# Hybrid encoder block on one core: operand sums and late low parts on GpSimd, query loads on ScalarE's queue

## Chip, core and metric

The kernel runs on one core of a Trainium2 chip. The metric is the device time of one execution in microseconds (us); smaller is better. Engines are named as in the profile: PE (TensorE matmuls), PEld (its weight loads), DVE (VectorE), ACT (ScalarE), POOL (GpSimd) and SP (SyncE, which only issues DMAs here).

## What is computed

One layer of a hybrid encoder on 2048 tokens of width 1024, all in float32:

```python
xn = rms_norm(h, ln_mix_g); proj = xn @ w_in
y_a = mlstm_group(...)          # 4 heads x 128, bidirectional, chunks of 128
y_b = mla_group(...)            # latent attention, 4 heads, scores 192 wide, values 128
h = h + concat([y_a, y_b]) @ w_out
u = dwconv3_centred(rms_norm(h, ln_ffn_g) @ w_up, conv_w, conv_b)   # 1024 -> 2 x 2816
gate, val = split(u); h = h + (silu(gate) * val) @ w_down            # 2816 -> 1024
gate = sigmoid(rms_norm(h, ple_norm_g) @ w_ple_gate)
h = h + gate * rms_norm(p @ w_ple_proj, ple_post_g)
out = rms_norm(h, final_g)
```

## The kernel before

Every float32 operand of a large product is split into a high part (ACT, `nc.scalar.copy` to fp32r, L117) and a low part (source minus high part, on DVE, L120). A product is three matmuls: low x high, high x low, high x high (`mm3`, L128, whose matmuls all carry the line L130).

The stages follow each other: the input projection; attention with the mLSTM interleaved as side work; the output projection; up and down; the per-layer input embedding (ple).

**Attention** (`attend_begin`, `attend`). 64 tiles of 128 queries, 16 for each head. A query tile pair (256 queries) is loaded from DRAM into `q_t` by `load_q` (L895), one of two places in turn, and split by `split_q`. The load is written at the start of an odd tile for the pair after next; its place is free when the last score matmul (L917) of the pair before has run. For a tile, five matmuls make each of four score banks, DVE takes their maxima (L918) and the maximum of those (`nm`, L929, L930), ACT the exponentials (L936), PE transposes them (L976), and they are split into `pt` for the product with the values. mLSTM work runs on all engines between these steps.

**Up and down** (`up_down`, L1376). Both products are done by a Strassen-Winograd scheme with seven products for a 2 x 2 block: A11 B11, S1 T1, S2 T2, A12 B21, S3 T3, A22 T4, S4 B22. A "pair" is one pass over these: 44 pairs for up (22 column blocks of gate and value, for two blocks of 1024 tokens), 24 for down (8 pairs of token tiles, for three blocks of the inner width). So there are five blocks; pairs 0, 22, 44, 52 and 60 begin one. The B and T operands (tile `op`, places x0 to x15) belong to a block and are loaded anew at its start by `load_op` (L1258): a DMA into one of six places t0 to t5 in turn (`opr`), then a split. B11, T1, T2, B21 and T3 are loaded during the last pair of the block before; T4 and B22 in the block's first pair, since the old ones are needed until then. Each has four parts (three in the last block).

The T operands are sums and differences of B parts. `sum4` (L1222) makes them: four loads (`tsum`, places t0 to t3), four subtractions (L1232 to L1235), and four stores to DRAM. `sums(0)` does this in the output projection for the first block of tokens and also splits three results in place; `sums(1)` for the second block of tokens (4 steps); `wsums` for the three blocks of w_down (11 steps).

In a pair the order is: A11 B11; S1 T1; `rest` of the pair before (A22 T4, then S4 B22); S2 T2; A12 B21; S3 T3. The results go through PSUM tiles `fxy` (x and y) and `fzs` (z and a spare bank): several products accumulate onto the same bank after DVE has added the partial result elsewhere (`add`, L1380), so PE waits for such additions. In up the results land in `ug` and `uv`, then `conv` (DVE, ACT) makes the gated hidden values, which go to DRAM. In down they are added into two output tiles `fh` (`s.o[0]`, `s.o[1]`), loaded by `down_out` from h1 or h2 in DRAM and stored back. Pair 44 (`NUP`), the first of down, takes its second output tile in the place `u2`, where `uv` of the last pair of up was.

**Last transposes.** The last token tile of the output projection is normalized (`norm_load`, L1070) and left pending; `turn(s, f)` (L1447) transposes half of it into the spare bank of a pair, copies it by ACT, and with the second half stores it to x2 in DRAM.

The program is written with a framework that assigns semaphores and, for the engines' queues, an order: it simulates the instructions with a cost model and takes the first ready one by the order of the text. So instructions can stand earlier in a queue than the text has them (the sums do), and each queue is then worked off strictly in that order, a waiting instruction holding up those behind it. All DMAs are issued by SP.

```python
if i == 1:
    turn(s, 1)
if prev:
    rest(prev)
...
if i == 0:
    turn(s, 0)
...
if i == NUP:
    c22 = self.at("t7", [P, SB], name="c22")
    add(c22, s.p1, s.y)
    add(c22, c22, s.z)
    s.o += self.down_out(NUP, (1,))
    add(s.o[1][:, L], s.o[1][:, L], s.p1)
    add(s.o[1][:, H], s.o[1][:, H], c22)
```

Of the kernel before, what the change touches and what calls it, by code (L numbers as in the profile page):

```python
# [14 lines left out]
ALU = mybir.AluOpType  # L15
# [33 lines left out]
def _f(ap):  # L49
    return ap.bitcast(F32)  # L50
# [10 lines left out]
class Block:  # L61
# [826 lines left out]
    def attend_begin(self):  # L888

        nc = self.nc  # L890
# [3 lines left out]

        def load_q(h, pr):  # L895
            q = self.at(f"w{4 - pr % 2}", [P, 4, 256], F32R, "q_t")
            nc.sync.dma_start(_f(q[:, 2:4]), self.q_d[h, pr])
            qv[h, pr] = q

        def split_q(h, pr):  # L900
# [293 lines left out]
    NUP = 2 * NC2  # L1194
# [27 lines left out]
    def sum4(self, src, dst, ops):  # L1222
        nc = self.nc
        r = []
        for i in range(4):
            r.append(self.at(f"t{i}", [P, SB], name="tsum"))
            nc.sync.dma_start(r[i], src(i))
        b11, b12, b21, b22 = r
        tt = nc.vector.tensor_tensor
        if ops:  # L1230
            self.split(b11, *ops["B11"])
        tt(b12, b12, b11, op=ALU.subtract)  # L1232
        tt(b22, b22, b12, op=ALU.subtract)
        tt(b11, b22, b11, op=ALU.subtract)
        tt(b21, b21, b22, op=ALU.subtract)  # L1235
        if ops:
            self.split(b12, *ops["T1"])
            self.split(b22, *ops["T2"])
        for i, t in enumerate((b12, b22, b11, b21)):
            if not ops or i > 1:  # L1240
                nc.sync.dma_start(dst(i), t)
# [16 lines left out]
    def load_op(self, blk, n):  # L1258

        ops = self.xop[n] = self.op_places(blk, n)  # L1260
        for k, (hi, lo) in enumerate(ops):
            raw = self.at(next(self.orot), [P, SB], name="opr")
            if blk < 2:
                if n[0] == "T":
                    src = self.t_d[blk, int(n[1]) - 1, :, k]
                else:
                    o = blk * 2 * SB + (int(n[2]) - 1) * SB
                    src = self.x2_d[:, (int(n[1]) - 1) * 4 + k, o:o + SB]
            elif n[0] == "T":
                src = self.tw_d[blk - 2, int(n[1]) - 1, :, k]  # L1270
            else:
                src = self.w_down(blk - 2, k, 2 * (int(n[1]) - 1) + int(n[2]) - 1)
            self.nc.sync.dma_start(raw, src)
            self.split(raw, hi, lo)

    def up_load(self, i):

# [98 lines left out]
    def up_down(self, out):  # L1376
# [19 lines left out]
        def rest(s):  # L1396

            prod(s.y, s.ops["A22"], "T4", True)
            if s.down:
                add(s.o[1][:, L], s.o[1][:, L], s.y)  # L1400
                nc.sync.dma_start(self.h2_d[2 * s.pr + 1], s.o[1])
            else:
                add(s.uv[:, 2:2 + SB], s.p1, s.y)
            prod(s.z, s.ops["S4"], "B22", True)
            if s.down:
                add(s.o[0][:, H], s.o[0][:, H], s.z)
                nc.sync.dma_start(self.h2_d[2 * s.pr], s.o[0])
            else:
                add(s.ug[:, 2 + SB:2 + 2 * SB], s.ug[:, 2 + SB:2 + 2 * SB], s.z)
# [37 lines left out]
        def turn(s, f):  # L1447

            xn, otag, dst = self.pending
            if f == 0:  # L1450
                self.pend_o = self.at(otag, [P, KT, P], name="nt_o")
            pt = s.spare.rearrange("p (k t) -> p k t", t=P)
            for j in range(4):
                kt = f * 4 + j
                nc.tensor.transpose(pt[:, j, :], xn[:, kt * P:(kt + 1) * P], self.ident)
            nc.scalar.copy(self.pend_o[:, f * 4:f * 4 + 4], pt)
            if f:
                nc.sync.dma_start(dst, self.pend_o)
# [6 lines left out]
        for i in range(n):  # L1465
# [32 lines left out]
            load(then, "T1")  # L1498
            side(7)
            if i == 1:  # L1500
                turn(s, 1)
            if prev:
                rest(prev)
            if j == 0 and blk:
# [4 lines left out]
            if s.down:  # L1509
                add(s.o[0][:, H], s.o[0][:, H], s.y)  # L1510
            else:
                s.ug = self.at(f"u{i % 2}", [P, 2 * SB + 2], name="ug")
                add(s.ug[:, 2 + SB:2 + 2 * SB], s.p1, s.y)
            if i == 0:
                load(0, "T3")
            load(then, "T2")
# [9 lines left out]
            else:  # L1526
                nc.scalar.copy(s.ug[:, 2:2 + SB], x)
            side(7)
            if i == 0:
                turn(s, 0)  # L1530
            if prev and not prev.down:
                conv(prev)
            if i == NUP - 1:
# [4 lines left out]
            if i == NUP:  # L1538
                c22 = self.at("t7", [P, SB], name="c22")
                add(c22, s.p1, s.y)  # L1540
                add(c22, c22, s.z)
                s.o += self.down_out(NUP, (1,))
                add(s.o[1][:, L], s.o[1][:, L], s.p1)
                add(s.o[1][:, H], s.o[1][:, H], c22)
                outs[i + 1] = self.down_out(i + 1)
            elif s.down:
                add(s.o[1][:, H], s.o[1][:, H], s.y)
                add(s.o[1][:, H], s.o[1][:, H], s.z)
            else:
                s.uv = self.at("u2", [P, 2 * SB + 2], name="uv")  # L1550
                add(s.uv[:, 2 + SB:2 + 2 * SB], s.p1, s.y)
                add(s.uv[:, 2 + SB:2 + 2 * SB], s.uv[:, 2 + SB:2 + 2 * SB], s.z)
# [198 lines left out]
```

## Time and profile before

| | us |
|---|---|
| median of 3 runs (2986.38 to 2987.69) | 2986.76 |
| profiled execution | 2983.04 |
| its span, first to last instruction | 2981.2 |
| PE busy | 2917.6 |
| DVE busy | 2068.2 |
| ACT busy | 1349.0 |
| POOL busy | 141.2 |

The span is 1.8 us shorter than the time of the same execution, which also holds what lies around it. The mean granted clock of TensorE is 0.997. Shares of busy time are means over stages with different limits; the waits of one engine for another and the time line of a stage tell what holds it up. The releaser named in a wait is the one that came last by the profile.

### The profile page before, as it was taken

To read this page: it belongs to the slowest core of one execution; us is meant where nothing else is said; L and a number is where in the kernel's file an instruction comes from. 1 tells how busy PE (TensorE), PEld (TensorE's weight loads), DVE (VectorE), ACT (ScalarE), POOL (GpSimd) and SP (SyncE) were. 2 spreads that over 40 slices of the span, in tenths; PEclk is the share of its full clock that TensorE was granted. 3 is DMA by queue.
4 is the path that set the end of the run, shared out by engine and by line. 5 is a ranking of instruction groups with operands and counts; after the bars stand their busy time and mean duration, and the time that the engine had idled before them with its cause. 6 is when DMAs were issued, how large, how long until landed. Compare 5 with 4: busy or idle time off the path is not lost. (4 is left out here: it accounts for less than half of the span.)

```text
span 2981.2 us, 40678 instructions
## 1 busy us (share of the span) xinstructions
PE 2917.6 (98%) x14858; PEld 2454.1 (82%) x14858; DVE 2068.2 (69%) x3799; ACT 1349.0 (45%) x2646; POOL 141.2 (5%) x262
## 2 busy tenths in 40 slices
PE   8999999999999999999999999999999999999999
PEld 7888888888898888888788888777887787877887
DVE  7431556777777777646798888877778777687565
ACT  7221545555665566523544445444445222233444
POOL 3100000000000000001000000000000000000111
PEclk9999999999999999999999999999999999999999
DMA  6522445343333343568663435786435556575221
GB/s 191 114 73 92 138 131 156 119 144 98 103 106 97 94 126 107 160 218 284 212 223 130 141 134 184 254 254 201 126 121 184 193 192 227 175 244 203 80 80 64
DMA packets 377400, 460.19 MB, mean 154 GB/s; under 512 B 30176, under 2 KB 263152, under 8 KB 377200
## 3 DMA queue, kind: packets, MB, share of 16 engines
q1 hardware_dynamic: 377200, 457.59, 48.1%
q8 instruction: 117, 1.92, 0.3%
q14 instruction: 83, 0.68, 0.1%
HBM read 294.26 MB, written 163.25 MB: 153 GB/s over the span
## 5 line engine op out<-in xcount | busy, mean ns | idle before, releaser
L130 PE MATMUL fxy<-op,fw 128*128 128x512 f32 x3168 | 752.8, 394 | 22.8 <-DVE fh L1380 13.0
L130 PEld LDWEIGHTS fxy<-op,fw 128*128 128x128 f32 x3168 | 588.3, 188 | 170.3 <-DVE fh L1380 23.4
L130 PE MATMUL fzs<-op,fw 128*128 128x512 f32 x1584 | 385.8, 389 | 0.8 <-DVE xt L1151 0.8
L130 PEld LDWEIGHTS fzs<-op,fw 128*128 128x128 f32 x1584 | 297.1, 188 | 63.0 <-DVE xt L1151 1.0
L130 PE MATMUL bk<-wsp,xh 128*128 128x512 f32 (+1 forms) x768 | 235.1, 387 | 1.0 <-DVE wsp L126 1.0
L117 ACT CAST pt<-tb 128x512 fp32r<-128x512 f32 x256 | 146.4, 586 | 194.2 <-PE tb L976 193.7
L918 DVE TENSOR_REDUCE mx<-bk 128x1 f32<-128x512 f32 x256 | 174.5, 684 | 45.4 <-PE bk L917 44.5
L130 PE MATMUL ppv<-pt,kv 128*128 128x256 f32 x1536 | 203.1, 287 | 0.0
L130 PE MATMUL fxy<-op,fwd 128*128 128x512 f32 x792 | 191.5, 390 | 6.0 <-DVE uv L1380 4.1
L120 DVE TENSOR_TENSOR pt<-tb,pt 128x512 fp32r<-128x512 f32 x256 | 173.7, 685 | 33.9 <-ACT pt L117 32.4
L130 PEld LDWEIGHTS ppv<-pt,kv 128*128 128x128 f32 x1536 | 188.7, 191 | 0.4 <-ACT pt L117 0.4
L936 ACT ACTIVATE pe<-bk,nm 128x512 f32<-128x512 f32 x256 | 174.2, 695 | 25.4 <-DVE nm L930 24.4
L130 PEld LDWEIGHTS fxy<-op,fwd 128*128 128x128 f32 x792 | 148.0, 188 | 39.0 <-DVE uv L1380 5.3
L130 PE MATMUL pgp<-pw,x3s 128*128 128x512 f32 (+1 forms) x792 | 178.5, 384 | 0.0
L130 PE MATMUL bk<-wo,yhl 128*128 128x512 f32 x744 | 175.6, 392 | 0.0
L130 PEld LDWEIGHTS bk<-wsp,xh 128*128 128x128 f32 x768 | 145.4, 190 | 27.3 <-DVE wsp L126 2.2
L130 PEld LDWEIGHTS pgp<-pw,x3s 128*128 128x128 f32 x792 | 144.5, 188 | 28.3
L1380 DVE TENSOR_TENSOR fh<-fh,fxy 128x512 f32<-128x512 f32 (+1 forms) x139 | 104.8, 768 | 86.0 <-PE fxy L130 84.8
L130 PEld LDWEIGHTS bk<-wo,yhl 128*128 128x128 f32 x744 | 138.2, 188 | 28.1
L130 PE MATMUL bk<-wsp,xl 128*128 128x512 f32 (+1 forms) x384 | 151.4, 394 | 7.9 <-DVE xl L120 7.9
L130 PE MATMUL bk<-xh,wqk 128*128 128x512 f32 x480 | 157.2, 393 | 0.0
L117 ACT CAST fw<-hraw 128x1024 fp32r<-128x1024 f32 (+1 forms) x72 | 70.3, 980 | 184.8 <-PE fxy L130 116.1
(331 smaller groups left out, 5020.5 us busy)
## 6 DMA issues: line engine op xcount, KB each, us to landing
fwr<-in_w_up SPq DMA_DIRECT2D x66, 512.0 KB, 4.2
fh<-h_d SPq DMA_DIRECT2D x48, 512.0 KB, 4.8
h_d<-fh SPq DMA_DIRECT2D x48, 512.0 KB, 2.8
s_d<-fwr SPq DMA_DIRECT2D x44, 512.0 KB, 3.2
fws<-s_d SPq DMA_DIRECT2D x44, 512.0 KB, 3.9
rw<-row_d SPq DMA_DIRECT2D x32, 512.0 KB, 5.1
hraw<-hid_d SPq DMA_DIRECT2D x30, 512.0 KB, 4.7
tsum<-in_w_down SPq DMA_DIRECT2D x44, 256.0 KB, 4.0
```

Of the source, the lines that this page charges most:

```text
L117: nc.scalar.copy(hi, src)
L120: (sub or nc.vector).tensor_tensor(lo, src, _f(hi), op=ALU.subtract)
L130: mm = lambda *a, **k: self.nc.tensor.matmul(*a, **k, skip_group_check=more)
L918: nc.vector.tensor_reduce(s.mx[:, kb:kb + 1], ps, axis=AX.X, op=ALU.max)
L936: nc.scalar.activation(s.pe[:, kb % 2], s.banks[kb], AF.Exp, bias=s.nm, scale=ASCALE, accum_out=s.rs[:, kb:kb + 1])
L1380: add = lambda o, a, b: tt(o, a, b, op=ALU.add)
```

## The change

Five parts. (a) `load_q` issues its DMA from ACT in place of SP. (b) The subtractions of `sum4` run on GpSimd, except those of `sums(0)`. (c) The low parts of T4 and B22 are made on GpSimd in all blocks but the first. (d) The two halves of the last transposes move from pair 0 (after A12 B21) and pair 1 (after S1 T1) to pair 1, after S1 T1 and after S2 T2. (e) In pair 44 the second output tile is no longer added to in the pair itself: in `rest`, DVE adds the product A22 T4 to `p1`, and GpSimd adds `p1` and `c22` to the two halves of the tile, which is then stored.

```diff
         def load_q(h, pr):
             q = self.at(f"w{4 - pr % 2}", [P, 4, 256], F32R, "q_t")
-            nc.sync.dma_start(_f(q[:, 2:4]), self.q_d[h, pr])
+            nc.scalar.dma_start(_f(q[:, 2:4]), self.q_d[h, pr])
...
-        tt = nc.vector.tensor_tensor
+        tt = (nc.vector if ops else nc.gpsimd).tensor_tensor
...
-            self.split(raw, hi, lo)
+            self.split(raw, hi, lo, sub=self.nc.gpsimd if blk and n in ("T4", "B22") else None)
...
             prod(s.y, s.ops["A22"], "T4", True)
-            if s.down:
+            if s.i == NUP:
+                add(s.p1, s.p1, s.y)
+                for f, t in ((L, s.p1), (H, s.c22)):
+                    nc.gpsimd.tensor_tensor(s.o[1][:, f], s.o[1][:, f], t, op=ALU.add)
+                nc.sync.dma_start(self.h2_d[1], s.o[1])
+            elif s.down:
                 add(s.o[1][:, L], s.o[1][:, L], s.y)
...
             if i == 1:
-                turn(s, 1)
+                turn(s, 0)
             if prev:
                 rest(prev)
...
                 add(s.ug[:, 2 + SB:2 + 2 * SB], s.p1, s.y)
+            if i == 1:
+                turn(s, 1)
...
             side(7)
-            if i == 0:
-                turn(s, 0)
...
                 add(c22, c22, s.z)
                 s.o += self.down_out(NUP, (1,))
-                add(s.o[1][:, L], s.o[1][:, L], s.p1)
-                add(s.o[1][:, H], s.o[1][:, H], c22)
+                s.c22 = c22
                 outs[i + 1] = self.down_out(i + 1)
```

## The prediction

> **What bounds the kernel now.** I read the page's busy times first, then the waits of PE, longest first, then busy times by stage, then the time line around the stages in which PE stands idle.
>
> ```profile
> span 2981.2 us, 40678 instructions
> PE 2917.6 (98%) x14858; PEld 2454.1 (82%) x14858; DVE 2068.2 (69%) x3799; ACT 1349.0 (45%) x2646; POOL 141.2 (5%) x262
> ```
>
> PE is idle for 2981.2 - 2917.6 = 63.6 us. The change removes no matmul, so that is all it can win, apart from clock. Who ends the idle time (total, times, longest):
>
> ```profile
> PE fxy L130 <- DVE fh L1380: 13.3, 8, 4.7
> PE fxy L130 <- DVE ug L1380: 6.2, 5, 1.8
> PE bk L913 <- ACT pe L936: 4.6, 4, 2.6
> PE fxy L130 <- DVE fw L120: 2.4, 1, 2.4
> PE fzs L1455 <- DVE xt L1070: 2.0, 1, 2.0
> ```
>
> The rows with fxy and fzs are up and down, where DVE empties the banks of PSUM; bk L913 is attention. In stages (busy us of PE, PEld, DVE, ACT, POOL, then the granted clock):
>
> ```profile
> 1432.00:1850.00 418.00, 415.20 (x1818) 336.95 (x1818) 352.12 (x454) 194.70 (x262) 0.73 (x2) 1.00 0.50 170
> 1850.00:1900.00 50.00, 43.94 (x189) 34.71 (x188) 44.81 (x60) 27.60 (x41) 0.00 (x0) 1.00 0.78 255
> 1900.00:2050.00 150.00, 143.13 (x621) 115.15 (x620) 122.63 (x158) 61.79 (x81) 0.00 (x0) 1.00 0.78 250
> 2050.00:2250.00 200.00, 200.00 (x881) 164.78 (x880) 145.39 (x170) 88.87 (x115) 0.00 (x0) 1.00 0.42 130
> 2250.00:2340.00 90.00, 80.15 (x336) 64.34 (x335) 78.38 (x108) 45.45 (x68) 0.00 (x0) 0.96 0.66 211
> 2340.00:2742.00 402.00, 396.80 (x1727) 319.80 (x1726) 298.58 (x418) 116.64 (x158) 1.49 (x5) 1.00 0.61 204
> 1024.00:1036.20 12.20, 11.76 (x68) 10.36 (x69) 8.25 (x23) 7.66 (x25) 1.20 (x2) 0.86 0.33 98
> 2332.60:2343.50 10.90, 10.90 (x41) 8.64 (x42) 7.96 (x10) 2.10 (x2) 0.00 (x0) 0.85 0.76 254
> ```
>
> In the first block of up (1432 to 1850) DVE is busy for 352.12 of 418 us, 84%, and PE loses 2.8 us. Between 1850 and 2050 DVE is as busy, 167.4 of 200 us, and PE loses 6.06 + 6.87 = 12.9. A high load of DVE alone does not stop PE; that DVE stands still, or does its work in the wrong order, does. PE is idle for 9.85 us from 2250 to 2340 (the first pairs of down) and for 5.2 after that. The last two rows begin at or near the end of a PE gap of 2.58 and 3.57 us (quoted below). Their granted clock is 0.86 and 0.85, so such a gap costs another 12.2 x 0.14 = 1.7 or 10.9 x 0.15 = 1.6 us.
>
> **Query loads on ScalarE's queue.** SP issues this load, 32 times, behind whatever its queue holds. Once it came late:
>
> ```profile
> 1016.55 0.32 SPq L812 DMA_DIRECT2D rw<-row_d  x1
> 1017.08 0.32 SPq L897 DMA_DIRECT2D q_t<-q_d  x1
> 1023.30 0.40 ACT L117 CAST q_t<-q_t 128x256 fp32r<-128x256 f32 x1 [3.19 <-DMA q_t<-q_d]
> 1024.44 0.50 PE L913 MATMUL bk<-kv,q_t 128*128 128x512 f32 x1 [2.58 <-ACT pe L936]
> ```
>
> All waits of ACT for it, all landings that the trace tells, and ACT's waits for the scores' maximum nm:
>
> ```profile
>   DMA q_t<-q_d: 8.0, 8
> DMA to landing us min/median/max: 2.4/2.6/4.9
> ACT pe L936 <- DVE nm L930: 24.4, 31, 1.8
> ```
>
> The load landed 6.2 us after its issue, against a median of 2.6, one place behind a larger transfer of the same queue. ACT stood at the cast of q_t, the exponentials behind it came late, and PE waited 2.58 us. In all ACT waits 8.0 us for this load. If all four waits of bk L913 (4.6 us) have this cause and the clock's 1.7 is added, 6.3 us can be won. Against it stands ACT's own time: 0.32 us an issue on SP, x 32 = 10.2 us at the most. Most of it falls where ACT waits anyway, 24.4 us in 31 cases, for nm before the first exponential of a tile; without that cover it would delay the exponentials one for one. The load waits for the last score matmul of a tile; queued behind it on ACT are the casts of the probabilities and the mLSTM activations, for which DVE and PE wait. The next exponential needs that matmul too, so the wait is short. SP's queue loses that wait, and its mLSTM loads go out earlier. Bounds: -6.3 to +10.2; I take -4.0, nearer to the row that shows the loss. The Trainium skill ("DMA: Bandwidth & Descriptors", Issuing engines are not separate DMA queues) says that DMAs of all issuing engines run on the same 16 DMA engines and that another engine saves only the time to initiate them. By that rule this term is about zero and the sum 4 us higher; no run here has a load on ACT's queue.
>
> **Last transposes moved.** PE's 2.0 us at fzs L1455 go: at pair 1 the normalized rows are long there, and PE passes at once to the next product. What is late next: the store of x2 goes out 36 matmuls, some 8 us, later, and loads for the sums queued behind it on SP wait for its landing; they are wanted only at pair 21. -2.0, with +2 as the other bound should a weight load be queued behind that wait.
>
> **Sums by way of DRAM on GpSimd.** 4 + 11 steps of 4 subtractions, 60 in all, leave DVE. Its waits for them, between 1432 and 2750, and the duration of one:
>
> ```profile
> DVE tsum L1232 <- DMA tsum<-in_w_down: 6.8, 4, 3.8
> DVE tsum L1232 <- DMA hid_d<-fgv: 3.7, 1, 3.7
> DVE tsum L1233 <- DMA tsum<-in_w_down: 2.8, 2, 2.0
> DVE tsum L1235 <- DMA tsum<-in_w_down: 1.6, 2, 0.9
> L1233 DVE TENSOR_TENSOR tsum<-tsum x19: 681/685/695, 1358.6 to 2042.2; 128x512 f32<-128x512 f32 x19
> ```
>
> One case in the time line, and PE behind it:
>
> ```profile
> 2042.18 0.69 DVE L1233 TENSOR_TENSOR tsum<-tsum 128x512 f32<-128x512 f32 x1 [2.04 <-DMA tsum<-in_w_down]
> 2047.13 1.21 PE L130 MATMUL fxy<-op,fwd 128*128 128x512 f32 x4 [1.32 <-DVE uv L1380]
> ```
>
> DVE stands still 14.9 us for loads (6.8 + 3.7 + 2.8 + 1.6), and with it the additions that free the banks. On GpSimd only GpSimd waits. Of the 6.87 us from 1900 to 2050 I take back 5.0. The results are needed at the next block, over 100 us later, so a slower GpSimd is hidden here.
>
> **Low parts of T4 and B22 on GpSimd.** 8 + 8 + 8 + 6 = 30 subtractions leave DVE at the four changes of block. There they stand ahead of additions that PE needs:
>
> ```profile
> 1869.52 3.69 DVE L120 TENSOR_TENSOR op<-opr,op 128x512 fp32r<-128x512 f32 x6
> 1873.13 0.68 DVE L1380 TENSOR_TENSOR ug<-p,fxy 128x512 f32<-128x512 f32 x1
> 1873.86 0.96 PE L130 MATMUL fxy<-op,fw 128*128 128x512 f32 x3 [1.16 <-DVE ug L1380]
> ```
>
> and, in the first pair of down,
>
> ```profile
> 2306.84 1.28 DVE L120 TENSOR_TENSOR op<-opr,op 128x512 fp32r<-128x512 f32 x2
> 2308.04 0.68 DVE L1380 TENSOR_TENSOR fh<-fh,fxy 128x512 f32<-128x512 f32 x1
> 2308.78 10.22 PE L130 MATMUL fxy<-op,fw 128*128 128x512 f32 x36 [4.72 <-DVE fh L1380]
> ```
>
> One takes 3.69 / 6 = 0.615 us in a row. At 1869 all six are of this kind: the gap of 1.16 goes, and half of the 2.4 us for fw, behind two others: -2.4. At 2306, by the order of the loads, three are: 3 x 0.615 brings the gap from 4.72 to 2.9: -1.8. In the later blocks (5.2 us idle) I take -1.0.
>
> **The first pair of down.** Its second output tile is loaded late, and DVE waits for it:
>
> ```profile
> 2330.61 0.69 DVE L1380 TENSOR_TENSOR fh<-fh,p 128x512 f32<-128x512 f32 x1 [1.44 <-DMA fh<-h_d]
> 2331.83 1.27 DVE L1380 TENSOR_TENSOR fh<-fh,fxy 128x512 f32<-128x512 f32 x2
> 2332.56 2.92 PE L130 MATMUL fxy<-op,fw 128*128 128x512 f32 x6 [3.57 <-DVE fh L1380]
> ```
>
> After the change DVE adds the product to p1, which needs no load, and GpSimd adds to the tile. Without the wait of 1.44 and the two additions ahead (2 x 0.615) the bank is free 2.7 us earlier; the rest of the gap is DVE's order, of which I take 0.4. With the clock's 1.6: -4.7. The tile's store goes out a little later, and is read a block later.
>
> **What GpSimd costs DVE.** 92 additions or subtractions run there (60 + 30 + 2). Before, it ran one operation of this size, with one tensor read, and DVE ran against it:
>
> ```profile
> L835 DVE TENSOR_TENSOR qi<-qk,rw x32: 664/916/1048, 659.8 to 1197.0; 128x512 f32<-128x512 f32 x32
> L830 POOL TENSOR_SCALAR_AFFINE_SELECT mk<-rw x32: 634/638/1168, 663.4 to 1195.7; 128x512 f32<-128x512 f32 x32
> ```
>
> Each slows the other: 664 becomes 1048 ns, 634 becomes 1168. With two tensors GpSimd's operation lies between 0.64 us and twice that, 1.28; I take 1.2. A DVE operation behind it then loses up to 0.38 + 0.56 = 0.94 us, against 0.615 saved; nothing when DVE is idle or, as I assume, has one of its inputs in PSUM. For 32 of the 92, at changes of block, the excess is 32 x 0.33 = 10.4 us at the most, and I charge half, 5.0. For the 60 sums it is 60 x 0.33 = 20 us spread over up, where DVE has 16% free; I charge 3.0. Bounds: 0 to 30. The Trainium skill ("SBUF — State Buffer", on the engine ports) says that a DVE instruction with two SBUF inputs and a GpSimd instruction that reads SBUF exclude each other for the whole instruction, that the later one blocks, and that a DVE instruction with only one SBUF input does not contend; the two rows agree with the first, and none of them shows the last. Its "GPSIMD Engine Reference" (Performance versus the Vector engine) advises DVE for elementwise work and gives 4497 ns for 2048 columns, from which 1.12 us for 512 is an estimate; by it the charge would be slightly smaller.
>
> **The sum.** -4.0 - 2.0 - 5.0 - 2.4 - 1.8 - 1.0 - 4.7 = -20.9; + 8.0; so about -13.0 us. The profiled execution took 2983.04 us (span 2981.2) and should take 2970.0 (span 2968.2). The median of the runs is 2986.76, 3.7 above the profiled one: 2973.8.
>
> **Rivals.** (1) *The low parts come late.* T4 and B22 are wanted one pair later, some 72 matmuls, at 200 us / 881 = 0.227 us, 16.3 us. Eight on GpSimd take 8 x 1.2 = 9.6; if each waits behind a DVE operation (0.68) they take 15.1, and with landing and cast they are late. It decides from about 1.9 us each. At 3 us late in four changes of block, with the clock's 1.6 each, it costs 18.4, and the 5.2 won there are lost: -13.0 + 23.6 = +10.6, 2997.4, slower. For it: 1168 is measured for one input. Against it: half of DVE's work there reads PSUM. (2) *The blocking eats the gain.* With all of the 20.9 charged in place of 8 (the bound is 30) the time is 2986.8, no change. For it: 1048 against 664 when the two meet. Against it: 84% load of DVE cost PE nothing in the first block. (3) *Hardly any blocking*, and the query loads win all: -20.9 - 2.3 = -23.2, 2963.6. (4) *The queue of ACT brings nothing* (the same DMA engines, the same landing): 2977.8, inside the forecast.
>
> **Numbers.** Forecast (with 4) 0.56, (1) 0.16, (2) 0.17, (3) 0.11. A measurement tells 0.2%, 6 us, from no change. Faster: 0.56 + 0.11 = 0.67; same 0.17; slower 0.16. The range is 2963.5 to 2990: it leaves out (1) and the far end of (3).
>
> **What would show it.** Right: no PE wait at L1455; no DVE wait on tsum; PE's gap near 2332 under 1 us; POOL's busy time up by 92 x 1.2 = 110 us; ACT's wait for q_t near zero. Wrong: POOL operations of 2 us and more with PE waiting for op behind them; DVE subtractions of 1.2 us in place of 0.69 in up; new waits of bk on ACT in attention.

## The result, and the profile after

| | before | after |
|---|---|---|
| median of runs side by side, us | 2986.57 (2982.27 to 2987.69) | 3034.72 (3029.95 to 3039.51) |
| profiled execution, us | 2983.04 | 3031.74 |
| its span, us | 2981.2 | 3029.9 |

The change makes the kernel slower: the ratio of after to before is 1.0164, interval 1.0143 to 1.0185, some 48 us where 13 us less were forecast. The parts of the change keep the letters of the section on the change: (a) query loads, (b) sums, (c) low parts, (d) last transposes, (e) first pair of down.

The first part of the page of after:

```profile
span 3029.9 us, 40705 instructions
PE 2940.3 (97%) x14858; PEld 2469.4 (82%) x14858; DVE 2069.9 (68%) x3707; ACT 1349.1 (45%) x2646; POOL 298.4 (10%) x354
```

DVE has 92 instructions less and is busy for as long as before (2068.2). POOL is busy for 157.2 us more; over 92 operations that is 1.7 us each. PE stands idle for 3029.9 - 2940.3 = 89.6 us, 26.0 more than before, and is itself busy for 22.7 us more with the same 14858 matmuls. The second goes with the clock. The slow spell behind one gap of PE, of which more below (length, busy us of PE, PEld, DVE, ACT, POOL, granted clock, DMA share, GB/s):

```profile
1485.43:1488.84 3.41, 3.41 (x10) 2.63 (x9) 0.47 (x2) 0.19 (x1) 0.02 (x1) 0.50 0.94 319
```

After a gap of 3.61 us the clock is 0.50 for 3.41 us and then full again (1.00 from 1488.84 on), which costs 1.7 us. So the clock adds to what such a gap costs.

The stages below are bounded by the same matmuls before and after, counted by their number. After: attention, the first block of up, and the part of the second block in which the sums for down are made; then the last two before:

```profile
479.68:1237.85 758.17, 741.30 (x4926) 664.53 (x4925) 551.06 (x1399) 452.00 (x1212) 44.16 (x62) 0.99 0.36 114
1437.89:1871.81 433.92, 422.35 (x1817) 340.92 (x1816) 354.31 (x438) 193.76 (x262) 30.56 (x18) 0.98 0.48 163
1925.19:2092.45 167.26, 149.47 (x621) 119.95 (x619) 113.59 (x116) 60.96 (x80) 61.55 (x39) 0.95 0.71 232
```

```profile
1432.14:1849.96 417.82, 415.02 (x1818) 336.81 (x1817) 352.08 (x454) 194.66 (x262) 0.73 (x2) 1.00 0.50 170
1900.11:2050.02 149.91, 143.04 (x620) 115.08 (x619) 122.52 (x158) 61.79 (x81) 0.00 (x0) 1.00 0.78 250
```

Against before: attention +6.1 us, first block of up +16.1, the change to the second block +3.2, the sums for down +17.4, the first pairs of down +1.3 and the rest of down +4.7. The two large ones are where the sums run on POOL (30.56 and 61.55 us busy). In the rest of up POOL does nothing, and it took as long as before (199.7 us).

The waits of PE after:

```profile
PE fxy L130 <- ACT ug L1534: 18.6, 8, 4.9
PE fxy L130 <- DVE uv L1380: 10.7, 3, 4.3
PE bk L913 <- ACT pe L936: 9.1, 5, 2.9
```

The wait at the transposes (L1455 before) is gone, as intended. No row says that PE waits for an operand that GpSimd made. What PE waits for is VectorE's and ScalarE's emptying of PSUM, later than before. There are two ways to this. The first, by VectorE, shows at the gap named above:

```profile
1475.06 1.30 POOL L1232 TENSOR_TENSOR tsum<-tsum 128x512 f32<-128x512 f32 x1 [34.01 <-DMA tsum<-x_d]
1475.95 3.71 DVE L1428 SCALAR_TENSOR_TENSOR fgv<-uv,fcw,fgv 128x1024 f32<-128x1024 f32 x2 [2.76 <-ACT fgv L1426]
1476.43 2.15 POOL L1233 TENSOR_TENSOR tsum<-tsum 128x512 f32<-128x512 f32 x1
1478.66 2.15 POOL L1234 TENSOR_TENSOR tsum<-tsum 128x512 f32<-128x512 f32 x1
1479.59 2.31 DVE L120 TENSOR_TENSOR fw<-fwr,fw 128x1024 fp32r<-128x1024 f32 x1
1480.78 2.24 POOL L1235 TENSOR_TENSOR tsum<-tsum 128x512 f32<-128x512 f32 x1
1481.82 2.28 DVE L1434 TENSOR_TENSOR fgv<-fgv 128x1024 f32<-128x1024 f32 x1
1484.02 0.68 DVE L1380 TENSOR_TENSOR uv<-p,fxy 128x512 f32<-128x512 f32 x1
1484.76 4.08 PE L130 MATMUL fxy<-op,fwd 128*128 128x512 f32 x10 [3.61 <-DVE uv L1380]
```

The two engines take turns. DVE's subtraction fw, which makes a low part and took 1.22 us before, takes 2.31; GpSimd's subtraction, 1.30 alone, takes 2.15 to 2.24. Each record seems to hold the wait for the other engine's operation and then its own. Four operations of DVE (two at L1428, fw, and L1434) end some 3 us late, and behind them on DVE stands the addition that frees PE's bank. The addition itself, with one input in PSUM, keeps its 0.68 us.

The second way, by SP's queue and ScalarE, is behind the largest row, ACT ug: 18.6 us, 1.1 before. Three of its waits (4.26, 4.90 and 4.26 us, at 1990, 2016 and 2064) lie in the second block of up. The last of them:

```profile
2038.07 1.22 DVE L1434 TENSOR_TENSOR fgv<-fgv 128x1024 f32<-128x1024 f32 x1
2050.53 2.29 POOL L1232 TENSOR_TENSOR tsum<-tsum 128x512 f32<-128x512 f32 x1 [6.21 <-DMA tsum<-in_w_down]
2052.85 0.33 SPq L1241 DMA_DIRECT2D tw_d<-tsum  x1
2053.23 0.42 SPq L1436 DMA_DIRECT2D hid_d<-fgv  x1
2057.66 1.24 ACT L1426 ACTIVATE fgv<-ug,fcw 128x1024 f32<-128x1024 f32 x1 [7.24 <-DMA hid_d<-fgv]
2063.47 0.58 ACT L1534 COPY ug<-fxy 128x512 f32<-128x512 f32 x1
2064.10 1.22 PE L130 MATMUL fxy<-op,fw 128*128 128x512 f32 x2 [4.26 <-ACT ug L1534]
```

The hidden values were ready at 2039.29. Their store (hid_d) stands in SP's queue behind a store of a sum, which goes out only when GpSimd's subtraction ends, at 2052.82; so it goes out 13.9 us after its data. ScalarE's next activation writes into the tile that is being stored and waits 7.24 us for the landing, and the copy ug that frees PE's bank stands behind it in ScalarE's order. The VectorE operations between that activation and the copy have their usual length. Before, every store of hidden values in up went out within 1.5 us of its data. At 1990 and 2016 ScalarE waits 5.09 and 4.99 us for the same kind of store, and stretched VectorE operations behind it add some 1.3 and 2.0 us.

### The profile page after: what moved, and what is told of

Same layout as the page of the kernel before. It is cut to its first block, busy times and chain, and to the rows that moved or that the text cites. A ratio compares the mean times of both kernels' runs of the same rounds, so it can differ in the third digit from the quotient of the medians.

```text
span 3029.9 us, 40705 instructions
## 1 busy us (share of the span) xinstructions
PE 2940.3 (97%) x14858; PEld 2469.4 (82%) x14858; DVE 2069.9 (68%) x3707; ACT 1349.1 (45%) x2646; POOL 298.4 (10%) x354
## 5 line engine op out<-in xcount | busy, mean ns | idle before, releaser
L130 PE MATMUL fxy<-op,fw 128*128 128x512 f32 x3168 | 766.8, 399 | 39.8 <-ACT ug L1534 18.6
L130 PEld LDWEIGHTS fxy<-op,fw 128*128 128x128 f32 x3168 | 598.3, 192 | 191.6 <-ACT ug L1534 26.4
L1380 DVE TENSOR_TENSOR fh<-fh,fxy 128x512 f32<-128x512 f32 (+1 forms) x138 | 103.9, 768 | 90.8 <-PE fxy L130 90.6
L1380 DVE TENSOR_TENSOR uv<-p,fxy 128x512 f32<-128x512 f32 x88 | 60.4, 686 | 139.7 <-PE fxy L130 139.7
```

The costliest lines, as they stand in the source:

```text
L130: mm = lambda *a, **k: self.nc.tensor.matmul(*a, **k, skip_group_check=more)
L1380: add = lambda o, a, b: tt(o, a, b, op=ALU.add)
```

## The experiments

The theory: operations of GpSimd and VectorE that both read from SBUF exclude one another, and the lost time collects ahead of VectorE's additions until PE stands still. The rivals: the moved results come late; the changed order of the instructions costs it; the loss comes from the parts that do not use GpSimd. Single profiles of kernels whose attention is untouched reach the start of up between 1.3 us earlier and 7.0 us later than before, so differences of a few us are taken from the ratios. The recorded expectations call VectorE's fw a product; it is the subtraction that makes a low part. Each ratio is against the kernel before on the same chip at the same time, where its median lay between 2981.21 and 2988.23 us.

### The parts one by one

(b) alone, from the kernel before:

```diff
-        tt = nc.vector.tensor_tensor
+        tt = (nc.vector if ops else nc.gpsimd).tensor_tensor
```

> The kernel before with one part alone: the 60 subtractions of the sums by way of DRAM on GpSimd. Blocking theory (a GpSimd subtraction and a DVE instruction with two SBUF inputs exclude each other for their whole length, every time they meet): 30 to 36 us slower, nearly all of it between the pairs in which the sums run (17 us in the first block of up, 17 in the second, as in the changed kernel), with DVE instructions of 2.2 us in place of 1.2, and 10 or more new spells of half clock. Planner theory (the changed kernel is slow because its queues are ordered otherwise): within 5 us of before, since PE's order here differs from before in few places. Late-operand theory (GpSimd's results come too late): no loss, since these results are wanted over 100 us later; about 5 us faster.

Measured: 3022.65 us, ratio 1.0125 (1.0102 to 1.0149), +37 us. It is the bulk of the loss.

(c) alone:

```diff
-            self.split(raw, hi, lo)
+            self.split(raw, hi, lo, sub=self.nc.gpsimd if blk and n in ("T4", "B22") else None)
```

> The kernel before with one part alone: the 30 low parts of T4 and B22 on GpSimd. Blocking theory: 6 to 10 us slower, at the changes of block, with PE waiting for DVE additions that stand behind blocked DVE subtractions. Late-operand theory: the same or more, 8 to 18 us, with PE waiting for GpSimd's op parts themselves. My forecast's own terms: 5 us faster without blocking.

Measured: 2996.17 us, ratio 1.0036 (1.0023 to 1.0049), +11 us. Time line of this kernel at the first change of block:

```profile
1868.38 9.67 POOL L120 TENSOR_TENSOR op<-opr,op 128x512 fp32r<-128x512 f32 x5 [430.54 <-DMA opr<-t_d]
1868.47 2.27 DVE L120 TENSOR_TENSOR fw<-fwr,fw 128x1024 fp32r<-128x1024 f32 x1
1871.26 1.18 DVE L120 TENSOR_TENSOR fwd<-fwr,fwd 128x512 fp32r<-128x512 f32 x1
1872.36 2.30 DVE L120 TENSOR_TENSOR fw<-fws,fw 128x1024 fp32r<-128x1024 f32 x1
1874.59 0.68 DVE L1380 TENSOR_TENSOR ug<-p,fxy 128x512 f32<-128x512 f32 x1
1875.32 0.97 PE L130 MATMUL fxy<-op,fw 128*128 128x512 f32 x3 [2.42 <-DVE ug L1380]
```

Three low parts of DVE (fw, fwd, fw) take 5.75 us in place of some 3.1, and ug is late by that.

The parts without GpSimd's sums and low parts, (a), (d) and (e), from the kernel after (the two additions of (e) stay on GpSimd):

```diff
-        tt = (nc.vector if ops else nc.gpsimd).tensor_tensor
+        tt = nc.vector.tensor_tensor
-            self.split(raw, hi, lo, sub=self.nc.gpsimd if blk and n in ("T4", "B22") else None)
+            self.split(raw, hi, lo)
```

> The changed kernel without the sums and without the low parts on GpSimd: query loads on ScalarE's queue, last transposes in pair 1, first pair of down as changed. If the losses add up: attention 5 to 6 us slower, transposes 1 to 2 us faster, first pair of down 0 to 5 us faster; together -1 to +5 us against before. Planner theory: 15 us slower or more, since its queues differ from before in more places than those of the other two.

Measured: 2996.75 us, ratio 1.0041 (1.0027 to 1.0055), +12 us. So without (b) and (c) the change is slower than before too.

(a) alone:

```diff
-            nc.sync.dma_start(_f(q[:, 2:4]), self.q_d[h, pr])
+            nc.scalar.dma_start(_f(q[:, 2:4]), self.q_d[h, pr])
```

> The kernel before with one part alone: the query loads on ScalarE's queue. Overtaking theory (SP no longer stands at the query load, so the two 512 KB row loads are in flight beside it and it lands later; ACT stands longer at the cast of q_t): about 6 us slower, with PE waits for the exponentials of 8 to 10 us in attention against 4.6 before. Issue theory (ACT's own time for 32 issues): 3 to 10 us slower, without longer waits for the landing. Forecast: 4 us faster.

Measured: 2989.89 us, ratio 1.0019 (1.0009 to 1.0029), +6 us (2.7 to 8.7). ScalarE's wait for q_t is 17.3 us, 8.0 before, and PE's wait at bk L913 10.0, 4.6 before.

### What it is in GpSimd's work that costs

The 60 subtractions of (b) replaced by fills, which write and read nothing:

```diff
+        fill = lambda o: [nc.gpsimd.memset(o, 0.0) for _ in range(3)]
...
+            tt(o, a, b, op=ALU.subtract) if ops else fill(o)
```

> The kernel before with part (b) alone, but each of the 60 GpSimd subtractions is replaced by three GpSimd fills of the same 128x512 tile, which write it and read nothing (the sums are left out, so the T operands of the later blocks are zero). Theory one (GpSimd and VectorE exclude one another while both read two operands from SBUF): with nothing read on GpSimd, VectorE's products fw and fgv stay near 1.22 to 1.28 us, and the loss of +37.8 us of the subtractions goes: 2982 to 2992 us. Rival (the sums simply come later from a slow engine, or GpSimd's being occupied delays what stands behind it): the fills take as long, so 3000 us or more, with VectorE's products at their old length and PE waiting for the operands. A third way: writes exclude as well, products at 1.7 us or more and 3010 us or more.

Measured: 2986.59 us, ratio 1.0003 (0.9994 to 1.0013). The whole loss is gone, with GpSimd busy for 89 us. Instructions between 1430 and 2300 us (count: min/median/max in ns, first and last start in us): first (b) alone, then with the fills.

```profile
L120 DVE TENSOR_TENSOR fw<-fwr,fw x85: 1211/1224/2305, 1433.4 to 2293.5; 128x1024 fp32r<-128x1024 f32 x85
L1233 POOL TENSOR_TENSOR tsum<-tsum x15: 1273/1674/2160, 1462.2 to 2036.8; 128x512 f32<-128x512 f32 x15
```

```profile
L120 DVE TENSOR_TENSOR fw<-fwr,fw x85: 1216/1223/1227, 1436.8 to 2262.5; 128x1024 fp32r<-128x1024 f32 x85
L1232 POOL MEMSET tsum<- x180: 519/527/548, 1447.8 to 2010.4; 128x512 f32 x180
```

With the fills no fw is stretched (1227 ns at most). A GpSimd that is as busy but reads nothing costs nothing in sum. This does not rule out the second way, since the stores of the sums wait for the fills too: the table below comes back to it.

Half of each subtraction, in the very order of TensorE's instructions that (b) has:

```diff
+                o, a, b = (x[:, :SB // 2] for x in (o, a, b))
```

> The kernel before with part (b) alone, the 60 GpSimd subtractions on the first 256 of 512 columns only (half of each sum is left out); the order of TensorE's instructions is that of the full-width version. Exclusion: a subtraction takes about 0.65 us alone, VectorE's products that meet it take about 1.9 us in place of 2.3, the sums' loss falls to about half or less: +8 to +19 over before, 2994 to 3005 us. If the loss is mostly a threshold (TensorE gaps over 2.5 us bring the half clock): it falls to under a third, under 2999 us, with few half-clock spells more than before. If the loss comes from the changed order of the instructions and not from the length of the subtractions: +30 or more, as at full width.

Measured: 2996.45 us, ratio 1.0032 (1.0017 to 1.0047): +10 us where the full width costs 37. Half the length costs a quarter, so the loss grows faster than the length: probably a bank freed a little late costs nothing, and a longer gap of PE also brings the half clock. Since the order is the same, the order alone is not the cause.

```profile
L120 DVE TENSOR_TENSOR fw<-fwr,fw x85: 1212/1224/1744, 1435.8 to 2273.7; 128x1024 fp32r<-128x1024 f32 x85
L1235 POOL TENSOR_TENSOR tsum<-tsum x60: 723/981/1804, 1463.3 to 2020.1; 128x256 f32<-128x256 f32 x60
```

Operations of one operand in place of the subtractions:

```diff
+            tt(o, a, b, op=ALU.subtract) if ops else nc.gpsimd.tensor_scalar(o, a, 1.0, None, op0=ALU.mult)
```

> Part (b) alone with the 60 subtractions on GpSimd replaced by multiplications of one operand by 1 in place (the sums are left out). If two operands are what excludes: VectorE's products at 1.22 to 1.28 us between 1430 and 2100, 2982 to 2992 us as with the fills. If any read on GpSimd excludes: products at 1.35 us or more in the mean and 3010 us or more, as with the subtractions.

Measured: 3006.86 us, ratio 1.0059 (1.0044 to 1.0074), +18 us: neither of the two expectations, between them.

```profile
L120 DVE TENSOR_TENSOR fw<-fwr,fw x85: 1211/1224/1632, 1438.6 to 2280.6; 128x1024 fp32r<-128x1024 f32 x85
L1233 POOL TENSOR_SCALAR tsum<-tsum x60: 1488/1510/2502, 1452.5 to 2024.5; 128x512 f32<-128x512 f32 x60
```

The fw of VectorE that meets it takes 1632 ns at most: 0.41 us more, not 1.09, although this operation is longer (1488 ns at least against 1273). So "two operands" in the expectation was too narrow: one operand read holds up VectorE as well, for a part of the operation. So short a delay hardly explains +18 us; the second way does.

The two ways in these kernels: waits between 1430 and 2300 us of the profiles, in us. PE waits for VectorE's additions (ug and uv, L1380 before) and for ScalarE's copy ug; ScalarE's activations wait for the store of the hidden values.

| kernel | PE for VectorE | PE for ScalarE's ug | sum of the two | ScalarE for the store | time against before |
|---|---|---|---|---|---|
| before | 10.3 | 1.1 | 11.4 | 0 | |
| fills | 3.4 | 8.3 | 11.7 | 15.4 | +1 |
| half width | 6.7 | 10.5 | 17.2 | 17.9 | +10 |
| one operand | 3.3 | 17.1 | 20.4 | 44.5 | +18 |
| (b) | 14.1 | 20.6 | 34.7 | 33.2 | +37 |

The time follows the sum of PE's two waits. With one operand the excess is all in the second way. With the fills PE waits less for VectorE and as much more for ScalarE. Only the full subtractions of two operands bring both. Stretched VectorE operations lengthen the second way too, as at 1990 and 2016. How the 37 us divide between the ways stays open: no run keeps the subtractions and moves the store of the hidden values ahead.

The same for (c), in the very order of (c) on TensorE, VectorE and ScalarE:

```diff
-        (sub or nc.vector).tensor_tensor(lo, src, _f(hi), op=ALU.subtract)
+        (sub or nc.vector).tensor_tensor(lo, src, _f(hi), op=ALU.subtract) if sub is None else sub.tensor_scalar(lo, src, 1.0, None, op0=ALU.mult)
```

> Part (c) alone, in its very order of instructions on TensorE, VectorE and ScalarE, but GpSimd's 30 subtractions of two operands are replaced by multiplications of one operand by 1 into the same tile (the high part is not taken off, so the low parts are wrong). If two operands read from SBUF are what excludes VectorE: VectorE's products beside them keep 1.22 to 1.28 us, the GpSimd operation does not stretch, and the run is within 4 us of the kernel before: 2982 to 2989 us. If the low parts come late because GpSimd is the slower engine (about 1 us an operation against 0.69): the TensorE gaps at 1921, 1986 and 2319 stay, 2992 to 2998 us. If any read on GpSimd excludes: as with two operands, 2996 us.

Measured: 2996.11 us against 2988.23 for before in the same session, ratio 1.0025 (1.0014 to 1.0036). The interval overlaps that of (c), so this run alone does not part exclusion from lateness. The fills go further:

```diff
+        nc.vector.tensor_tensor(lo, src, _f(hi), op=ALU.subtract) if sub is None else [sub.memset(_f(lo), 0.0) for _ in range(3)]
```

> Part (c) alone with each of the 30 GpSimd subtractions replaced by three fills of the same tile (0.53 us each), which read nothing and wait for no data (the low parts are zero). If reads on GpSimd are what costs (exclusion, in whole or in part): within 3 us of the kernel before. If the work taken from VectorE changes the order for the worse, or GpSimd's being occupied delays the operands: 6 us or more slower, as with one operand read.

Measured: 2978.66 us against 2987.74, ratio 0.9973 (0.9963 to 0.9983): faster than before by 8 us. Taking the low parts from VectorE does free time there; GpSimd's reads take it back, and 11 us more. It is no version to use, since it leaves out the low parts of T4 and B22. What it does not settle: the fills wait for no load, so how much of (c)'s loss is exclusion and how much an operand that is ready later stays open.

### The last transposes

(d) alone:

```diff
             if i == 1:
-                turn(s, 1)
+                turn(s, 0)
...
+            if i == 1:
+                turn(s, 1)
...
-            if i == 0:
-                turn(s, 0)
```

> The kernel before with part (d) alone, the last transposes in up's second pair. The prediction's term was -2.0 us, the store of the last columns counted as hidden. Theory now: the store comes some 7 to 8 us later against TensorE's work, the loads of the sums that read those columns wait for it on the queue of SP, VectorE's subtractions wait for the loads in order, and TensorE for VectorE's additions behind them: +5 to +9 us, all of it between 1470 and 1540 us, with a TensorE gap of 3 us or more there: 2990 to 2994 us. Rival (the term of the prediction): 2983 to 2986 us.

Measured: 2990.81 us against 2981.21, ratio 1.0032 (1.0020 to 1.0044), +10 us. In its profile the loss, 7.4 us, lies between 1470 and 1540. Waits there, of VectorE and of PE:

```profile
DVE tsum L1233 <- DMA tsum<-x_d: 4.1, 1, 4.1
DVE tsum L1232 <- DMA tsum<-x_d: 2.0, 1, 2.0
PE fxy L130 <- DVE ug L1380: 3.8, 1, 3.8
```

The same without the dependency: the sums read other columns, which the late store does not write.

```diff
-            src = lambda i: self.x2_d[:, k + i // 2 * 4, t0 + i % 2 * SB:t0 + i % 2 * SB + SB]
+            src = lambda i: self.x2_d[:, k + i // 2 * 4, t0:t0 + SB]
```

> The same, part (d) alone, but the sums read columns 1024 to 1535 twice in place of 1024 to 2047 (so those for the second block of up are of other data), and thus no longer wait for the store of the last columns. Theory: the wait of VectorE for these loads and the TensorE gap are gone, and the run comes out within 3 us of the kernel before: 2982 to 2988 us. Rival (the transposes themselves, or the changed order, cost it in the second pair): as the run before, 2990 us or more.

Measured: 2985.45 us against 2981.21, ratio 1.0010 (1.0000 to 1.0019).

```profile
DVE tsum L1232 <- DMA tsum<-x_d: 0.5, 1, 0.5
DVE tsum L1233 <- DMA tsum<-x_d: 0.4, 1, 0.4
```

The long wait of VectorE and PE's gap are gone, and with them some two thirds of the loss. The store of the last columns was not hidden: the loads of the sums wait for it, VectorE for the loads, and VectorE works in order.

### The query loads

The split of a query tile written later in the text of a tile:

```diff
-            if qt % 2 == 0 and i + 2 < len(seq):
-                split_q(seq[i + 2][0], seq[i + 2][1] // 2)
...
+                    if qt % 2 == 0 and i + 2 < len(seq):
+                        split_q(seq[i + 2][0], seq[i + 2][1] // 2)
```

> The kernel before with one step moved: the cast and the subtraction that split a query tile stand at the end of a tile of attention in place of its beginning; the query loads stay on the queue of SP. If ScalarE's in-order wait for the query load is what delays the exponentials behind it: ScalarE's wait for q_t falls from 8.0 us to under 2, TensorE's wait for the exponentials from 4.6 us to under 2, and the run is 3 to 5 us shorter, 2982 to 2984. Rival: the split now ends too late for the next tile's scores, TensorE waits for the query tile instead, 2986 to 2992.

Measured: 2988.62 us, ratio 1.0013 (1.0002 to 1.0024): a miss. ScalarE waits for q_t 11.0 us, where it is 8.0 before and 7.7 to 10.8 in kernels with untouched attention; the cast stands close behind the load in ScalarE's order again.

A third buffer:

```diff
-            q = self.at(f"w{4 - pr % 2}", [P, 4, 256], F32R, "q_t")
+            place = f"w{4 - pr % 2}" if h == NH - 1 else ("w4", "w3", "w13")[(h * 8 + pr) % 3]
+            q = self.at(place, [P, 4, 256], F32R, "q_t")
```

> The kernel before with a third buffer for the query tiles (13th work area, free during attention but for the last head, which keeps two buffers); the loads stay on the queue of SP. Theory: what holds a query load is not a queue but its buffer: the 8 loads whose tile ScalarE waits for are issued 0.02 us after TensorE's last read of the buffer. With a third one ScalarE's wait for q_t falls from 8.0 us to under 2, TensorE's wait for the exponentials from 4.6 to under 2: 3 to 5 us less, 2980 to 2983 us. Rival (ScalarE's waits there hide behind TensorE's work, or other waits take their place): 2984 to 2988 us.

Measured: 2982.25 us against 2981.21, ratio 1.0003 (0.9994 to 1.0013): a miss too. ScalarE's wait for q_t is 8.8 us. Loads and casts both move forward by a pair of tiles, and the cast stands behind the load as before.

(a) with the row loads on ScalarE's queue as well (first edit), and the kernel before with the row loads on GpSimd's queue (second edit):

```diff
-                nc.sync.dma_start(rw.rearrange("p h a t -> p (h a t)"), ...
+                nc.scalar.dma_start(rw.rearrange("p h a t -> p (h a t)"), ...
```

```diff
-                nc.sync.dma_start(rw.rearrange("p h a t -> p (h a t)"), ...
+                nc.gpsimd.dma_start(rw.rearrange("p h a t -> p (h a t)"), ...
```

> Part (a) with the loads of the rows rw (512 KB each) on ScalarE's queue as well, so that they stand behind the query load again. Theory: part (a) cost 4 us because the query load lost its place ahead of the row loads; where both start at one moment, it landed in up to 5.9 us and not 3 to 3.7. Then its landings fall to under 4.5 us at the places where ScalarE waits, ScalarE's wait for q_t from 17.3 to under 10 us, and the run to 2984 to 2988 us. Rival (the issue on ScalarE itself costs it, 0.33 us each and the wait for TensorE's last read in order): 2990 us or more, since 32 more issues stand there.

> The kernel before with the loads of the rows rw issued from GpSimd's queue, the query loads on SP as before; the order of TensorE's instructions is that of before. Theory of the lost place: the row loads no longer stand behind the query load, so the query load lands later where they meet, ScalarE's wait for q_t rises from 8.0 us to 12 or more, and the run is 2 to 5 us longer than before, though ScalarE issues nothing: 2986 to 2990 us. Rival (ScalarE's part in the issue is the cost): within 1.5 us of before.

Measured: with both on ScalarE's queue 2989.01 us against 2988.23, ratio 1.0000 (0.9990 to 1.0010); with the rows on GpSimd's queue 2989.73, ratio 0.9999 (0.9989 to 1.0008). One load in the time lines of four kernels. Before:

```profile
1090.17 0.32 SPq L897 DMA_DIRECT2D q_t<-q_d  x1
1090.60 1.63 SPq L812 DMA_DIRECT2D rw<-row_d  x2
1093.44 0.41 ACT L117 CAST q_t<-q_t 128x256 fp32r<-128x256 f32 x1 [0.41 <-DMA q_t<-q_d]
```

(a) alone:

```profile
1093.85 1.75 SPq L812 DMA_DIRECT2D rw<-row_d  x2
1093.86 0.35 ACTq L897 DMA_DIRECT2D q_t<-q_d  x1
1099.82 0.40 ACT L117 CAST q_t<-q_t 128x256 fp32r<-128x256 f32 x1 [3.57 <-DMA q_t<-q_d]
```

Rows on GpSimd's queue:

```profile
1092.01 0.32 SPq L897 DMA_DIRECT2D q_t<-q_d  x1
1092.48 0.61 POOL L812 DMA_DIRECT2D rw<-row_d  x1
1097.97 0.40 ACT L117 CAST q_t<-q_t 128x256 fp32r<-128x256 f32 x1 [3.17 <-DMA q_t<-q_d]
```

Both on ScalarE's queue:

```profile
1090.25 0.33 ACTq L897 DMA_DIRECT2D q_t<-q_d  x1
1093.69 0.41 ACT L117 CAST q_t<-q_t 128x256 fp32r<-128x256 f32 x1 [1.04 <-DMA q_t<-q_d]
```

The cast follows the issue by 3.27 us where the row loads (512 KB each) stand behind the query load on one queue, by 5.96 us in both cases where they come from another queue at the same time, and by 3.44 us where they share ScalarE's queue; there they go out only at 1097.89. So on SP's queue the query load had been ahead of the row loads here, and (a) took that place away. That the time follows is shown less well. With both on ScalarE's queue its wait for q_t is 10.9 us, not 17.3, and the loss is gone, so the time for issuing on ScalarE is not what costs. With the rows on GpSimd's queue the wait rose to 12.6 us, as expected but little above the scatter, and the run did not get longer, which was not expected.

### The first pair of down, and the best pieces

(e) alone, with its additions on VectorE:

```diff
+            if s.i == NUP:
+                add(s.p1, s.p1, s.y)
+                for f, t in ((L, s.p1), (H, s.c22)):
+                    nc.vector.tensor_tensor(s.o[1][:, f], s.o[1][:, f], t, op=ALU.add)
```

> The kernel before with part (e) alone, the two additions of the first pair of down on VectorE and not GpSimd. The prediction's term: the TensorE gap of 2.7 us near 2332 and its half clock go, -2.7 to -4.7 us: 2982 to 2984. Rival (the order of other instructions shifts and eats it): 2985 to 2989.

Measured: 2981.12 us against 2985.17, ratio 0.9988 (0.9977 to 0.9999). PE's wait for fh between 2300 and 2345, before and with (e):

```profile
PE fxy L130 <- DVE fh L1380: 8.3, 2, 4.7
```

```profile
PE fxy L130 <- DVE fh L1380: 4.7, 2, 4.0
```

The gap near 2332, 3.57 us before, is 0.78 there.

(e) with the third query buffer, and (e) with query and row loads on ScalarE's queue:

> Part (e) with its additions on VectorE, together with the third query buffer. If both gains hold and add, 3.6 us from the one and 3 to 5 us from the other: 2976 to 2980 us. If the buffer brings nothing, as part (e) alone: 2980 to 2983 us.

> Part (e) with its additions on VectorE, and part (a) with the row loads on ScalarE's queue behind the query loads. (e) alone was 3.6 us faster, the pair of loads was no slower than before: if they add, 3 to 6 us under the kernel before. Rival (what is left is within the scatter of the kernel): within 2 us of before.

Measured: 2981.73 us against 2981.21, ratio 1.0000 (0.9990 to 1.0011), and 2987.30 against 2987.74, ratio 1.0003 (0.9995 to 1.0012). Nothing adds. (e) alone is the only version with the whole computation whose interval lies below before, and by no more than its edge; in these two runs, which hold it as well, its gain cannot be told from none.

## Why the prediction was wrong, step by step

**What GpSimd costs DVE** is the step that failed. It charged 8.0 us, with a bound of 30. For the sums alone, (b) costs 37 us and the fills 1; for (c), the way from the fills to the subtractions is 8 + 11 = 19 us, part of which may be lateness. Its parts:
- The duration of one operation was nearly right (1.2 taken, 1.27 to 1.30 measured alone). The loss of a VectorE operation that meets it was put at up to 0.94 us and measures 1.09 (1.22 to 2.31).
- It was then spread thin: "DVE has 16% free; I charge 3.0". Free time in a stage's mean is no cover for a series. The sums come four in a row; each of them can catch the next operation of VectorE, and the delays add up in front of one addition that PE waits for (3.61 us at 1484).
- A second way to PE was put at nothing, in the term of the sums: "The results are needed at the next block, over 100 us later, so a slower GpSimd is hidden here." PE waits for none of the results, but their stores hold up SP's queue, the store of the hidden values behind them is late, ScalarE waits for it, and PE for ScalarE's ug (18.6 us in all in the profile after, 1.1 before).
- The clock was charged in no term of the blocking. With 22.7 us of the 48.7 by which the span grew, PE's longer busy time is nearly half.

What was assumed about inputs in PSUM held: such additions stay at 0.68 us beside GpSimd's subtractions. The Trainium skill ("SBUF — State Buffer", on the engine ports), which the prediction cited, says that the later of the two operations blocks for the whole of the other. The rows of the subtractions agree (2.15 to 2.31 us, in turns). Those with one operand do not: no fw took more than 1632 ns beside GpSimd operations of 1488 ns or more.

**Sums on GpSimd**, -5.0: about right for VectorE, and taken back elsewhere. With the fills VectorE has neither these subtractions nor their waits, and PE's waits for VectorE's additions fall by 6.9 us (10.3 to 3.4); but its waits for ScalarE's ug rise by 7.2 (1.1 to 8.3), and the time is that of before (1.0003).

**Low parts**, -5.2: the sign and about the size were right, -8 us with the fills, as far as these stand for a GpSimd that costs nothing.

**Query loads**, -4.0: +6 us measured, within the bounds of -6.3 to +10.2. The step that failed is the reading of the row at 1017: the load came late "one place behind a larger transfer of the same queue", and another queue was to free it. But what holds the load is its buffer. The queue of SP in attention before (waited for, us, times, longest):

```profile
SPq L897 <- PE bk L917: 111.8, 25, 18.4
```

25 of the 32 loads wait for PE's last read of the buffer, which no queue makes earlier; (a)'s load at 1093.86 goes out right behind that read as well. What the queue of SP gave was the place ahead of the row loads, where the two meet as at 1090. The rule of the Trainium skill that the prediction cited, that all queues share the DMA engines ("DMA: Bandwidth & Descriptors"), gave this term as about zero, which is nearer than -4.0; the runs add that transfers of two queues then meet.

**Last transposes**, -2.0: PE's wait at the transposes is gone, but the term is +10 us alone. The step that failed: "they are wanted only at pair 21". The operands are; the subtractions that make them stand in VectorE's queue at once, ahead of the additions that PE waits for.

**The first pair of down**, -4.7: right in kind, -3.6 us (-6.9 to -0.3).

**The sum.** The parts alone give 37 + 11 + 6 + 10 - 4 = 60 us, the change as a whole 49. Those without GpSimd's work add up (6 + 10 - 4 = 12, and 12 measured together), so the overlap is between them and the rest. One overlap has a reason in the trace: with (b), GpSimd and not VectorE waits for the late store, and VectorE has no wait on tsum in the profile after. That this is the 11 us was not tried.

**The rivals.** That the low parts come late, as rival (1) had it, is not shown: no wait of PE names one that GpSimd made. That its time (2997.4 us) lay within 2 us of that of (c) alone is chance. Rival (2), the blocking, was the mechanism in part, at 20.9 us far too small; that the sums' stores hold up SP's queue was no rival. Of the signs named, right were the missing waits at L1455 and on tsum; signs of being wrong that came: POOL operations above 2 us (though no wait of PE for op names them) and longer waits of bk on ScalarE (9.1 us against 4.6). ACT's wait for q_t, named as near zero, is 15.6 us in the profile after. POOL's busy time rose by 157 us, not 110.

## What to carry to other kernels

Before work goes to GpSimd beside a busy VectorE, look at which VectorE operations have all their inputs in SBUF: a GpSimd operation with two operands that meets one costs nearly its own length (1.09 of 1.27 us here), and operations in series add up in front of the one addition that TensorE waits for, so the mean load of the stage says little. Look also at the DMA queue: a store that waits for a slow engine's result holds back the stores behind it, and whoever waits for those. A transfer or a store is hidden only if every engine that waits for its result in order has nothing urgent queued behind; and a load's place on a queue ahead of a larger one is worth something that another queue does not give. A gain of a few us shown by one profile of such a kernel is no gain until several runs say so.

## What the hardware showed that was not expected

- GpSimd fills of 128x512 (519 to 548 ns), 180 of them in 89 us, stretch VectorE's operations fw (1227 ns at most) and fgv (1287) not at all. A GpSimd operation with one operand read (1488 ns alone) stretches a VectorE subtraction of 128x1024 by up to 0.41 us, one with two (1273 ns alone) by up to 1.09.
- PE's clock goes to 0.50 for 3.41 us late in a gap or within about a microsecond of its end; behind the gap of 4.30 us at 1531 about twice as long (a mean of 0.82 over the 19 us from 1526). In the profile after, gaps from 1.89 us (at 1498) to 4.90 us (at 2016) did this; the gap of 2.40 us at 1869 before did not. The Trainium skill ("TensorE: Matmul & The Clock Gate", Part 1) has the clock halved after at least one idle window of about 3.4 us; the gap of 1.89 us is shorter than that.
- A VectorE copy of 128x2 from SBUF took 1.26 us in place of 0.16 while GpSimd made the low parts of (c), so that short copies are held up as well.
